# Hybrid attention/recurrence layer: attention's and the gates' loads on the GpSimd queue, tiles under store reused last, two heads' probability products at a time, the ranking held at the first pair

## The chip, the cores and the metric

The kernel runs on one core of a Trainium2 chip. The metric is device microseconds (us) of one execution, as a median over runs; the profile is of one further execution. The engines are named as in the profile: PE (matrix products), PEld (its weight loads), DVE (vector), ACT (scalar), POOL (GpSimd), SP (only issues transfers). ACT and POOL can issue transfers too; `SPq`, `ACTq` and `POOLq` in the profile are the issuing sides of these engines.

## What is computed

One layer over 512 tokens plus 16 prepended meta tokens, model width 2048, all in float32. Cut to what matters here:

```python
proj = rms_norm(x, norm_g) @ w_in                 # 2048 x 12368
(q_a, k_a, v_a, z_a, q_i, k_i, w_i, q_b, f_b, i_b, z_b, gates) = split(proj)
# branch A: an indexer scores keys, the best 128 per query are kept, 8 heads attend to them
score = einsum(relu(qi . ki), wi);  sel = top_k(score, 128)
o_a = softmax(q . k over sel) @ v;  y_a = o_a * silu(z_a)      # 8 heads, 4 key/value groups
# branch B: gated linear recurrence, 8 heads
y_b = rms_norm(hgrn2(silu(q_b), f, i_b)) * silu(z_b)
p = einsum('btnc,ncd->btnd', stack(y_a, y_b), w_branch)
out = x + sum(sigmoid(gates) * p, n) @ w_out
```

## The kernel before

**Products in three parts.** Each float32 operand is split into a high and a low part (`hi_lo`, L381: ACT copies the high part, DVE subtracts for the low one), and each product is three matmuls: high x high, high x low, low x high. In the profile `wh`/`wl` are the parts of a weight, `hH`/`hL` of the normed input, `yH`/`yL` of a branch's output.

**Stages.** First the indexer's columns and four of branch B's gate columns run as plain jobs (`pg`, about the first 196 us). Then pairs of column blocks run in a seven-product scheme (`run_pair`, L1306, with banks `px`, `py`, `pz`, `pw`), one pair in about 20 us. Seven operands per pair are prepared on the side: sums of weight blocks on DVE (`sum_1`, `sum_2`, L408) and by accumulating transfers on POOL (`sum_3`, `sum_4`, L419). The seven input operands include one, `t3`, that needs its own place in `hH`/`hL`: `place_t3` (L1286) copies it there when the last plain job has read them. Then 32 plain jobs multiply by `w_branch`: 16 for branch B (n=1), 16 for branch A (n=0), 24 matmuls each (`pg` again). The last stage multiplies by `w_out` with the seven-product scheme (`po`).

**Attention between the jobs.** The 8 heads of attention are worked off as side tasks between the matmuls of branch B's 16 jobs. `vs_task` (L791) prepares the meta tokens' values. `att_task(h)` (L851) loads a head's `qH`, `qL` and, for every second head, its group's four key/value tiles `kv`; forms the logits `plg`; adds the mask and takes the maximum on DVE (L895); takes the exponential and normalizes on ACT. It then starts `pv_task(h)` (L914): PE transposes blocks of probabilities (`ppt`), ACT and DVE split them (`pT`, `pTH`, `pTL`, `pS`), PE multiplies them with the values (`pov`). At its end a head is multiplied by its gate `za` and split into `yH[0,h]`, `yL[0,h]`, which the jobs of branch A read. A head's `pv_task` begins when those of all heads before it are done. Before the first job of branch A, `req_br` (L1557) runs the side tasks until all eight are done.

**What sets the order.** Nothing moves instructions after they are written. The Python code keeps an estimated clock per engine (`Core.at`, L57 on) and a list of tasks; `pump` (L222) is called after every few matmuls and steps any task whose time has come by that clock. Tasks have priorities; the ranking, `topk_task` (L679: 16 rounds for each of four query blocks), has number 6. Each engine takes its instructions in the written order, so an instruction that waits holds up all behind it on its engine. This goes for transfers as well: SP issues weight loads (`load_chunk`, L356), spills, the attention's loads and the gates' loads in one row.

**Memory.** 69 slots of 128 x 528 are handed out by `Slots.get`, which takes the free one whose last use by the estimated clock is the oldest. `Slots.put` (L167) frees a slot and notes that last use. A slot that is freed right after its store to DRAM was issued counts as last used by the computation before the store. The n=1 jobs' gates come back from DRAM (`load_gates`, L1468) into two weight tiles in turn; branch B's outputs come back by `load_y` (L1482), eight tiles, in the last pair.

Of the kernel before, what the change touches and what calls it, by code (L numbers as in the profile page):

```python
# [8 lines left out]
F32 = mybir.dt.float32  # L9
# [135 lines left out]
class Slots:  # L145
# [20 lines left out]

    def put(self, *aps):  # L167
        for a in aps:
            nm = a.tensor.name
            t = self.tag.pop(nm)  # L170
            self.last[t] = self.core.ac.get(nm, (0.0, "pe"))
            self.free.append(t)
# [9 lines left out]
def hybrid_kernel(ctx, tc, x, meta, vecs, w_in, rows, w_branch, w_out,  # L182
# [12 lines left out]

    tasks = []

# [24 lines left out]
    def pump(limit=3000.0):  # L222
        moved = True
        while moved:
            moved = False
            for t in list(tasks):
                now = E.clk["pe"]
                lim = limit if t.prio < 5 else 1200.0
                if t.t + MARGIN <= now and E.clk["dve"] < now + lim and E.clk["act"] < now + limit:
                    if not t.done and t.step():  # L230
                        moved = True
                        break
# [485 lines left out]
    def keep_out(moves, tiles, e, key):  # L718
        yield e
        for dst, src in moves:  # L720
            nc.sync.dma_start(dst, src if src.dtype == F32 else src.bitcast(F32))
        S.put(*tiles)
        stored.add(key)
# [67 lines left out]
    def vs_task():  # L791
        while len(stored) < 17:
            yield WAIT
        yield from room(8)
        vx3.extend((slot("vS", F32R), slot("pS", F32R), slot("v3")))
        vS, _, v3 = vx3
        nc.scalar.dma_start(v3[:, :512], v3d)
        vx = slot("vx")
        nc.scalar.dma_start(vx[:, :64], vxd)
        for t in vx3[:2]:  # L800
            E.pool([t], [], T // 2, lambda v: v.memset(t[:96, :512].bitcast(F32), 0.0))
# [15 lines left out]
    def spill(dst, s, e, key=None):  # L817
        yield e
        nc.sync.dma_start(dst, s[:, :512])
        S.put(s)  # L820
        if key:
            y_out.add(key)
# [28 lines left out]
    def att_task(h):  # L851
        g = h // 2
        while not vx3 or h and att.get(h - 1, 0) < 1 or not topk_done():
            yield WAIT
        yield from room(2 if g in kTH else 6, 6)
        if g not in kTH:
            for d, src, n in ((kTH, kd_[g][0], T), (kTL, kd_[g][1], T), (vH, vd_[g][0], 512), (vL, vd_[g][1], 512)):
                d[g] = slot("kv", F32R)
                nc.sync.dma_start(d[g][:, :n].bitcast(F32), src)
        qH, qL = slot("qH", F32R), slot("qL", F32R)  # L860
        for i, t in enumerate((qH, qL)):
            nc.sync.dma_start(t[:, :512].bitcast(F32), qd_[h][i])
        yield E.clk["pe"] + 7000.0
        while h and att[h - 1] < 2 or len(S.free) < 8:
# [23 lines left out]
        att[h] = 1  # L888
        yield e3
        col = lambda qt, i: sm[:, 4 * qt + i:4 * qt + i + 1]  # L890
# [10 lines left out]
        for qt in (3, 2, 1, 0):  # L901
            xs = ps[qt][:, :KQ[qt]]
            e = E.act(xs, xs, AF.Exp, bias=col(qt, 1), accum_out=col(qt, 2))
        yield e
        E.dve([sm], [sm], 4, lambda vv: vv.reciprocal(allc(3), allc(2)))
# [3 lines left out]
        att[h] = 2  # L909
        pv_tasks.append(spawn(pv_task(h, ps, e), 1))  # L910

    pv_tasks = []

    def pv_task(h, ps, e):  # L914
        g = h // 2
        gs = slice(128 * g, 128 * g + 128)
        for t in pv_tasks[:h]:
            while not t.done:
                yield WAIT
        yield e  # L920
        vS, pS, v3 = vx3
        po = yield from bank("pov")
# [17 lines left out]
        for b in (3, -1, 0, 1, 2):  # L940
# [14 lines left out]
            if b == 3:  # L955
                z = slot("za")
                nc.sync.dma_start(z[:, :512], zad[h])
            if b != 2:
# [15 lines left out]
        e = E.tt(z[:, :512], po, z[:, :512], OP.mult)  # L974
        B1.put(po)
        if h % 2 == 1:
            S.put(kTH[g], kTL[g], vH[g], vL[g])
# [328 lines left out]
    def run_pair(pr, nxt, late, last):  # L1306
# [3 lines left out]
        for i, (wn, tn, bn, on_) in enumerate(SEVEN):  # L1310
# [46 lines left out]
            if last:  # L1357
                if i == 1:
                    while len(y_out) < 8:
                        pump(1e9)  # L1360
                        if len(y_out) < 8:
                            E.clk["pe"] += 200
                    yr = load_y(0, 4)
                elif i == 3:
                    S.put(*hH[:8], *hL[:8])
                    yr += load_y(4, 8)
                    ysplit = split_y(yr, 1)
                elif i == 4:
                    S.put(*[t for k in range(8) for t in TB[k]["tiles"][:2]])
                elif i == 5:  # L1370
                    S.put(*[TB[k]["tiles"][2] for k in range(8)])
                elif i == 6:
                    S.put(*hH[8:], *hL[8:])
                    late.pop(0)()
                if i in (4, 5):
                    for _ in range(4):
                        next(ysplit, None)
# [90 lines left out]
    def load_gates(n, p):  # L1468
# [6 lines left out]
        for i in range(2):  # L1475
            nc.sync.dma_start(g[i][:, :512], gd[n][p + 8 * i])
            gate[n, p + 8 * i] = g[i]
# [3 lines left out]

    def load_y(a, b):  # L1482
        yr = slots("yr", b - a)
        for h in range(a, b):
            nc.scalar.dma_start(yr[h - a][:, :512], yd[h])
        return yr
# [58 lines left out]
    def d_gate(n, j, c0):  # L1545
        def f(g):
            E.act(g[:, c0:512], g[:, c0:512], AF.Sigmoid)
            nc.sync.dma_start(gd[n][j], g[:, :512])
            S.put(g)
        return f  # L1550
# [6 lines left out]
    def req_br(n, p):  # L1557
        def f():
            if p == 0:
                if n:  # L1560
                    load_gates(1, 0)
                else:
                    while len(pv_tasks) < 8 or not all(t.done for t in pv_tasks):
                        pump(1e9)
                        E.clk["pe"] += 200
            if p < 7:
# [9 lines left out]
    jobs[7].pre = lambda: spawn(consts(), 2)  # L1576
    jobs[-1].pre = lambda: (sum_1(jobs[ji]), sum_2(jobs[ji]))

# [105 lines left out]
    for k in E.clk:  # L1684
        E.clk[k] = max(E.clk[k], E.clk["pe"]) + (2500.0 if k in ("dve", "act") else 0.0)
    npair, late = 0, []
    first_out = min(i for i, j in enumerate(jobs) if j.kind == "out")
    for ji, job in enumerate(jobs[2:], 3):
# [5 lines left out]
        if job.kind == "pair":  # L1694
            npair += 1
            if npair == 1:
                for t in t_task:
                    finish(t)
                late += [lambda: place_t3(0), lambda: place_t3(4)]
            last = npair == len(pairs)  # L1700
# [17 lines left out]
        else:  # L1718
            b = B1.get("pg")
            parts = [(b[:job.ncols, :], slice(0, 512))]  # L1720
            if job.kind == "in":
                parts = [(b[:job.ncols, :].rearrange("p (a b) -> p a b", a=2), None)]
        for ch in job.chunks:
            split_upto(ch["prep"] + 2)
# [83 lines left out]
```

## Time and profile before

| | |
|---|---|
| median of 3 runs | 1540.3 us (1539.25 to 1540.68) |
| the profiled execution | 1538.31 us, of it the span from first to last instruction 1536.5 us |
| granted PE clock, mean | 0.996 |
| busy in the span | PE 1506.5, DVE 1177.3, ACT 683.3, POOL 156.9 us |
| transfers issued by POOL, by SP and by ACT | 52.52 MB (q0); 186.89 MB (q1); 8.69 MB (q10) |

How to read it: a row of a wait is "who waited on which line, for what: us in total, times, the longest". A row of a timeline is "start, duration, engine, line, operation, out<-in, count", and in brackets the idle time before it and what ended it. Busy times of PE overlap a little, since one matmul's modelled end lies behind the next one's start. "PEclk" is the share of full clock that was granted.

### The profile page before, as it was taken

How to read it: one execution, taken by the hardware profiler on the slowest of the kernel's cores; microseconds unless marked ns; L12 is line 12 of the kernel's file. 1: busy time of each engine (PE TensorE's matmuls, PEld its weight loads, DVE VectorE, ACT ScalarE, POOL GpSimd, SP SyncE). 2: the span in 40 equal slices, each digit the busy share in tenths (PEclk: the TensorE clock that was granted, in tenths of full speed). 3: DMA queues.
4: the chain of work that ended last, by engine and by line, in shares of the span. 5: the costliest groups of instructions: out<-in, count | busy, mean ns of one | idle time of the engine just before them, and what ended most of it. 6: DMA issues, size and time to landing. Idle time of an engine off the chain costs nothing.

```text
span 1536.5 us, 30975 instructions
## 1 busy us (share of the span) xinstructions
PE 1506.5 (98%) x12648; PEld 1423.1 (93%) x12648; DVE 1177.3 (77%) x1971; ACT 683.3 (44%) x1050; POOL 156.9 (10%) x162
## 2 busy tenths in 40 slices
PE   7999999999999999999999999999989999999998
PEld 6888899999999999999999999999987887889998
DVE  6799999999998778677768776886654555778775
ACT  5555444444444433443444344334465553334332
POOL 3100000001111101101000000000100000002222
PEclk9999999999999999999999999999999999999999
DMA  9323367777887855766676667566777543458873
GB/s 265 83 69 83 100 143 181 185 176 167 214 206 186 201 136 138 180 146 162 145 172 135 157 163 169 142 151 172 189 237 241 158 138 103 143 142 214 221 206 91
DMA packets 305999, 250.08 MB, mean 163 GB/s; under 512 B 13060, under 2 KB 268048, under 8 KB 305856
## 3 DMA queue, kind: packets, MB, share of 16 engines
q1 hardware_dynamic: 284448, 186.89, 41.6%
q0 software_dynamic: 14464, 52.52, 20.2%
q10 hardware_dynamic: 6944, 8.69, 1.7%
q8 instruction: 99, 1.62, 0.4%
q14 instruction: 44, 0.36, 0.1%
HBM read 168.00 MB, written 27.62 MB: 127 GB/s over the span
## 4 chain that ended last, share of the span: by engine, by line
PE 91%; DMA 3%; DVE 2%; ACT 2%; issue 2%; POOL 0%; SPq 0%; ACTq 0%; POOLq 0%; DVEq 0%
PE pg L93 20%; PE pz L91 15%; PE py L91 15%; PE px L91 14%; PE po L91 10%; PE pw L91 7%; PE phl L93 1%; PE psc L93 1%; PE plg L93 1%; PE pov L91 1%; PE pho L93 1%; DMA raw<-in_w_branch_dram 1%; DMA qL<-qd 1%; PE phs L93 1%; ACT wh L101 1%
## 5 line engine op out<-in xcount | busy, mean ns | idle before, releaser
L101 ACT ACTIVATE wh<-raw 128x1024 fp32r<-128x1024 f32 x304 | 322.3, 1060 | 479.1 <-PE pz L91 123.4
L107 DVE TENSOR_TENSOR wl<-raw,wh 128x1024 fp32r<-128x1024 f32 x302 | 371.5, 1230 | 142.2 <-ACT wh L101 140.6
L91 PE MATMUL px<-hH,wh 128*128 128x256 f32 (+1 forms) x672 | 193.8, 288 | 0.0
L91 PE MATMUL px<-hH,wl 128*128 128x256 f32 (+1 forms) x672 | 189.6, 282 | 0.0
L91 PE MATMUL px<-hL,wh 128*128 128x256 f32 (+1 forms) x672 | 189.1, 281 | 0.0
L101 ACT ACTIVATE wh<-sum 128x1024 fp32r<-128x1024 f32 x100 | 106.1, 1061 | 181.7 <-PE pw L91 72.6
L91 PE MATMUL po<-wh,mh 128*128 128x256 f32 x896 | 158.4, 280 | 0.5 <-DVE xq L107 0.5
L107 DVE TENSOR_TENSOR wl<-sum,wh 128x1024 fp32r<-128x1024 f32 x100 | 128.4, 1284 | 35.2 <-ACT wh L101 35.1
L91 PEld LDWEIGHTS po<-wh,mh 128*128 128x128 f32 x896 | 137.2, 189 | 0.8 <-DVE xq L107 0.7
L91 PEld LDWEIGHTS px<-hH,wh 128*128 128x128 f32 x672 | 126.4, 188 | 0.9
L91 PEld LDWEIGHTS px<-hL,wh 128*128 128x128 f32 x672 | 126.4, 188 | 0.0
L91 PEld LDWEIGHTS px<-hH,wl 128*128 128x128 f32 x672 | 126.4, 188 | 0.0
L91 PE MATMUL po<-wl,mh 128*128 128x256 f32 x448 | 125.5, 280 | 0.0
L91 PE MATMUL py<-tT,wh 128*128 128x256 f32 (+1 forms) x672 | 124.9, 285 | 0.0
L91 PE MATMUL pw<-tT,wh 128*128 128x256 f32 (+1 forms) x672 | 124.5, 284 | 0.0
L91 PE MATMUL pz<-tT,wh 128*128 128x256 f32 (+1 forms) x672 | 123.3, 283 | 0.0
L116 POOL DMA_DIRECT2D raw<-raw x50 | 43.2, 864 | 753.7 <-DVE sum L107 743.9
L91 PEld LDWEIGHTS py<-tT,wh 128*128 128x128 f32 x672 | 103.3, 188 | 0.5
L91 PEld LDWEIGHTS pw<-tT,wh 128*128 128x128 f32 x672 | 103.3, 189 | 0.2
L91 PEld LDWEIGHTS pz<-tT,wh 128*128 128x128 f32 x672 | 103.1, 188 | 0.2
L93 PE MATMUL pg<-yH,wh 128*128 128x512 f32 x256 | 102.7, 401 | 0.0
L93 PE MATMUL pg<-yH,wl 128*128 128x512 f32 x256 | 100.5, 393 | 0.0
(307 smaller groups left out, 3766.4 us busy)
## 6 DMA issues: line engine op xcount, KB each, us to landing
raw<-in_w_in_dram SPq DMA_DIRECT2D x192, 512.0 KB, 4.6
raw<-raw POOLq DMA_DIRECT2D x50, 512.0 KB, 5.3
raw<-sum POOLq DMA_DIRECT2D x50, 512.0 KB, 5.7
raw<-in_w_branch_dram SPq DMA_DIRECT2D x32, 512.0 KB, 4.7
raw<-in_w_out_dram SPq DMA_DIRECT2D x32, 512.0 KB, 4.6
gd<-g SPq DMA_DIRECT2D x32, 256.0 KB, 4.8
g<-gd SPq DMA_DIRECT2D x30, 256.0 KB, 3.0
x<-in_x_dram SPq DMA_DIRECT2D x16, 256.0 KB, 5.5
```

The costliest lines, as they stand in the source:

```text
L91: self.nc.tensor.matmul(out, lhsT, rhs, start=start, stop=stop, skip_group_check=True)
L93: self.nc.tensor.matmul(out, lhsT, rhs, start=start, stop=stop)
L101: self.nc.scalar.activation(out, in_, f, **kw)
L107: self.nc.vector.tensor_tensor(out, a, b, op=op)
L116: self.nc.gpsimd.dma_start(out, a, accum_op=OP.add)
```

## The change

- **Queues.** The attention's loads (`qH`, `qL`, `kv`, `za`, the meta tokens' `v3` and `vx`) and the gates' loads go from SP or ACT to POOL's queue; of `load_y`'s eight loads the first four stay on ACT and the other four go to POOL. A head's q is asked for ahead of its group's kv. The first gates of branch B (`load_gates(1, 0)`) are asked for at the end of the last pair.
- **Slots.** `put(..., late=9000.0)` counts a slot that is under a store as last used 9 us from now, so that `get` prefers others.
- **Two heads at a time.** There are two `pS` tiles, and a head's `pv_task` waits for the head before the last one only; the multiplication's end still keeps the order of heads. The written waits between a head's steps are longer: 10000 in place of 7000 (ns by the estimated clock) from its loads to its logits, 600 more ahead of the mask, 1200 ahead of the reciprocal, 1000 ahead of `pv_task`.
- **Branch A's start.** `req_br` waits for no head. The first two jobs of branch A run through the eight inner blocks together, and each block waits only for its own head.
- **First pair.** From the last plain job's start until the first pair's second product, tasks with a priority number over 5 are not stepped (`hold`); both halves of `place_t3` are written ahead of the pair and not after its first and second product.

```diff
-    def put(self, *aps):
+    def put(self, *aps, late=0.0):
...
-            self.last[t] = self.core.ac.get(nm, (0.0, "pe"))
+            w = self.core.ac.get(nm, (0.0, "pe"))
+            self.last[t] = (max(w[0], self.core.clk["pe"]) + late, "dma") if late else w
...
+                if t.prio > 5 and hold:
+                    continue
...
-        S.put(*tiles)
+        S.put(*tiles, late=9000.0)
...
-        vx3.extend((slot("vS", F32R), slot("pS", F32R), slot("v3")))
-        vS, _, v3 = vx3
-        nc.scalar.dma_start(v3[:, :512], v3d)
+        vx3.extend((slot("vS", F32R), slot("pS", F32R), slot("pS", F32R), slot("v3")))
+        vS, v3 = vx3[0], vx3[3]
+        nc.gpsimd.dma_start(v3[:, :512], v3d)
...
+        qH, qL = slot("qH", F32R), slot("qL", F32R)
+        for i, t in enumerate((qH, qL)):
+            nc.gpsimd.dma_start(t[:, :512].bitcast(F32), qd_[h][i])
...
-                nc.sync.dma_start(d[g][:, :n].bitcast(F32), src)
-        qH, qL = slot("qH", F32R), slot("qL", F32R)
-        for i, t in enumerate((qH, qL)):
-            nc.sync.dma_start(t[:, :512].bitcast(F32), qd_[h][i])
-        yield E.clk["pe"] + 7000.0
+                nc.gpsimd.dma_start(d[g][:, :n].bitcast(F32), src)
+        yield E.clk["pe"] + 10000.0
...
-        yield e3
+        yield e3 + 600
...
-        yield e
+        yield e + 1200
...
-        pv_tasks.append(spawn(pv_task(h, ps, e), 1))
+        pv_tasks.append(spawn(pv_task(h, ps, e + 1000), 1))
...
-        for t in pv_tasks[:h]:
-            while not t.done:
-                yield WAIT
+        while h > 1 and not pv_tasks[h - 2].done:
+            yield WAIT
...
-                nc.sync.dma_start(z[:, :512], zad[h])
+                nc.gpsimd.dma_start(z[:, :512], zad[h])
...
+        while h and not pv_tasks[h - 1].done:
+            yield WAIT
...
-                    yr = load_y(0, 4)
+                    yr = load_y(0, 4, nc.scalar)
...
-                    yr += load_y(4, 8)
+                    yr += load_y(4, 8, nc.gpsimd)
...
+                    load_gates(1, 0)
...
-            nc.sync.dma_start(g[i][:, :512], gd[n][p + 8 * i])
+            nc.gpsimd.dma_start(g[i][:, :512], gd[n][p + 8 * i])
...
-            if p == 0:
-                if n:
-                    load_gates(1, 0)
-                else:
-                    while len(pv_tasks) < 8 or not all(t.done for t in pv_tasks):
-                        pump(1e9)
-                        E.clk["pe"] += 200
...
-    jobs[-1].pre = lambda: (sum_1(jobs[ji]), sum_2(jobs[ji]))
+    jobs[-1].pre = lambda: (sum_1(jobs[ji]), sum_2(jobs[ji]), hold.append(1))
...
-                late += [lambda: place_t3(0), lambda: place_t3(4)]
+                place_t3(0)
+                place_t3(4)
+                late += [lambda: None, lambda: hold.clear()]
...
+        if job.kind == "br" and job.n == 0 and job.c0 in (0, 1024):
+            ahead.append((job, b))
+            if len(ahead) < 2:
+                continue
+            split_upto(ahead[1][0].chunks[0]["prep"] + 1)
+            for kt in range(8):
+                while (0, kt) not in yL or not pv_tasks[kt].done:
+                    pump(1e9)
...
+                for j, o in ahead:
+                    mm3(o, j.chunks[0], kt, kt, yH[0, kt][:, :512], yL[0, kt][:, :512], kt == 0, kt == 7)
+                    pump()
+            for j, o in ahead:
+                j.done(o)
+            continue
```

**What moves, place one: DVE at the first pair.** Before, from the first half of `place_t3` (`hL`) to the first pair's second product, whose subtraction from `py` is the row that begins with `p_`; MAX and MATCH_REPLACE are one round of the ranking, `tk` its work tile:

```order
L107 TENSOR_TENSOR hL_347<-t_148_1338,hH_346 128x264
L107 TENSOR_TENSOR hL_362<-t_148_1338,hH_361 128x264
L690 MAX m_0_2001<-tk_2000 128x8
L691 MATCH_REPLACE tk_2000<-m_0_2001,tk_2000 128x144
L690 MAX m_1_2009<-tk_2008 128x8
L691 MATCH_REPLACE tk_2008<-m_1_2009,tk_2008 128x272
L107 TENSOR_TENSOR p_253_2279<-p_253_2279,py_2298 128x256
L107 TENSOR_TENSOR wl_2330<-sum_26_2153,wh_2329 128x1024
L107 TENSOR_TENSOR hL_376<-t_105_1043,hH_375 128x264
```

Now, from the second half of `place_t3` on:

```order
L107 TENSOR_TENSOR hL_415<-t_236_2079,hH_414 128x264
L107 TENSOR_TENSOR hL_439<-t_236_2079,hH_438 128x264
L107 TENSOR_TENSOR wl_2252<-raw_2016,wh_2251 128x1024
L107 TENSOR_TENSOR wl_2284<-raw_1840,wh_2283 128x1024
L107 TENSOR_TENSOR p_253_2281<-p_253_2281,py_2292 128x256
L107 TENSOR_TENSOR wl_2320<-sum_26_2153,wh_2319 128x1024
L693 MAX m_0_2001<-tk_2000 128x8
L694 MATCH_REPLACE tk_2000<-m_0_2001,tk_2000 128x144
```

All eight `hL` stand ahead of the pair's weights, and nine rounds of the ranking, which stood between the last plain job and this subtraction, stand behind it.

**Place two: the queue that carries the first head's loads.** Before, on SP, the first head's loads among the loads of `w_branch` and the store of the gates:

```order
L363 DMA raw_13875<-in_w_branch_dram 128x8x128
L363 DMA raw_13908<-in_w_branch_dram 128x8x128
L859 DMA kv_13922<-kd_0_122 128x528
L859 DMA kv_13924<-kd_1_123 128x528
L859 DMA kv_13926<-vd_0_130 128x512
L859 DMA kv_13928<-vd_1_131 128x512
L862 DMA qH_13930<-qd_0_138 128x512
L862 DMA qL_13931<-qd_1_139 128x512
```

Now, on POOL, from the last accumulating transfer of the last pair on:

```order
L116 DMA raw_13559<-sum_190_13687 128x1024
...
L1490 DMA yr_13897<-yd_170 128x512
L800 DMA v_556_13909<-v3d 128x512
L802 DMA vx_13911<-vxd 128x64
L804 MEMSET vS_13906 96x512
L804 MEMSET pS_13907 96x512
L804 MEMSET pS_13908 96x512
L861 DMA qH_13916<-qd_0_138 128x512
L861 DMA qL_13917<-qd_1_139 128x512
L865 DMA kv_13920<-kd_0_122 128x528
L865 DMA kv_13922<-kd_1_123 128x528
```

The loads stand behind no weight load any more, but behind four `yr` loads, the meta tokens' loads and three fills. SP's row is 72 instructions shorter (473 to 401), POOL's 79 longer (167 to 246).

**Place three: PE at the end of attention.** Before, in head 6 (bank `pov_15281`), the second last:

```order
L91 MATMUL pov_15281<-pS_13760,vS_13759 128x512
L97 MATMUL ppt_15307<-ident,lg_14829 128x128
L97 MATMUL ppt_15307<-ident,lg_14827 128x128
L97 MATMUL ppt_15307<-ident,lg_14825 128x128
L91 MATMUL pov_15281<-pTH_15303,kv_14719 128x512
L91 MATMUL pov_15281<-pTL_15304,kv_14719 128x512
```

Now, with head 6 in bank `pov_15153` and the last head, 7, in `pov_15231`:

```order
L91 MATMUL pov_15153<-pTH_15224,kv_14810 128x384
L93 MATMUL pg_15211<-yH_13965,wh_14992 128x512
L93 MATMUL pg_15211<-yL_13966,wh_14992 128x512
L93 MATMUL pg_15211<-yH_13965,wl_14993 128x512
L93 MATMUL pg_15211<-yH_13969,wh_14992 128x512
L93 MATMUL pg_15211<-yL_13970,wh_14992 128x512
L93 MATMUL pg_15211<-yH_13969,wl_14993 128x512
L91 MATMUL pov_15231<-pS_13908,vS_13906 128x512
```

Before, heads 6 and 7 stood alone behind the last job of branch B. Now they alternate with each other and with that branch's fourteenth job, and two whole jobs (48 matmuls) stand behind the last head.

More of the change, by code (lines that the diff above doesn't have):

```diff
@@ L193, in hybrid_kernel @@
     B2 = Slots(E, pp, ["c0"], [128, 2, 512], None)
-    tasks = []
+    tasks, hold = [], []
     class Task:
@@ L793, in vs_task @@
             yield WAIT
-        yield from room(8)
-        vx3.extend((slot("vS", F32R), slot("pS", F32R), slot("v3")))
-        vS, _, v3 = vx3
-        nc.scalar.dma_start(v3[:, :512], v3d)
+        yield from room(9)
+        vx3.extend((slot("vS", F32R), slot("pS", F32R), slot("pS", F32R), slot("v3")))
+        vS, v3 = vx3[0], vx3[3]
+        nc.gpsimd.dma_start(v3[:, :512], v3d)
         vx = slot("vx")
-        nc.scalar.dma_start(vx[:, :64], vxd)
-        for t in vx3[:2]:
+        nc.gpsimd.dma_start(vx[:, :64], vxd)
+        for t in vx3[:3]:
             E.pool([t], [], T // 2, lambda v: v.memset(t[:96, :512].bitcast(F32), 0.0))
@@ L819, in spill @@
         nc.sync.dma_start(dst, s[:, :512])
-        S.put(s)
+        S.put(s, late=9000.0)
         if key:
@@ L916, in pv_task @@
         gs = slice(128 * g, 128 * g + 128)
-        for t in pv_tasks[:h]:
-            while not t.done:
-                yield WAIT
+        while h > 1 and not pv_tasks[h - 2].done:
+            yield WAIT
         yield e
-        vS, pS, v3 = vx3
+        vS, pS, v3 = vx3[0], vx3[1 + h % 2], vx3[3]
         po = yield from bank("pov")
@@ L1480, in hybrid_kernel, with load_y @@
     yH, yL = {}, {}
-    def load_y(a, b):
+    def load_y(a, b, q):
         yr = slots("yr", b - a)
         for h in range(a, b):
-            nc.scalar.dma_start(yr[h - a][:, :512], yd[h])
+            q.dma_start(yr[h - a][:, :512], yd[h])
         return yr
@@ L1548, in f @@
             nc.sync.dma_start(gd[n][j], g[:, :512])
-            S.put(g)
+            S.put(g, late=9000.0)
         return f
@@ L1685, in hybrid_kernel @@
         E.clk[k] = max(E.clk[k], E.clk["pe"]) + (2500.0 if k in ("dve", "act") else 0.0)
-    npair, late = 0, []
+    npair, late, ahead = 0, [], []
     first_out = min(i for i, j in enumerate(jobs) if j.kind == "out")
@@ L1722, in hybrid_kernel @@
                 parts = [(b[:job.ncols, :].rearrange("p (a b) -> p a b", a=2), None)]
+        if job.kind == "br" and job.n == 0 and job.c0 in (0, 1024):
[6 more added lines that the diff above has]
+                    pump(1e9)
+                    if (0, kt) not in yL or not pv_tasks[kt].done:
+                        E.clk["pe"] += 200
+                for j, o in ahead:
[4 more added lines that the diff above has]
+            continue
         for ch in job.chunks:
```

## The prediction, before the result was known

> **What bounds the kernel now.** First the page's busy times, then who PE waits for.
>
> ```profile
> PE 1506.5 (98%) x12648; PEld 1423.1 (93%) x12648; DVE 1177.3 (77%) x1971; ACT 683.3 (44%) x1050; POOL 156.9 (10%) x162
> PE pc L97 <- DMA vrow<-in_vecs_dram: 7.7, 1, 7.7
> PE plg L93 <- DMA qH<-qd: 7.3, 3, 4.4
> PE py L91 <- DVE p L107: 2.5, 1, 2.5
> PE pov L91 <- DVE pS L107: 2.1, 2, 1.2
> ...
> PE pz L91 <- DVE g L107: 0.7, 1, 0.7
> ```
>
> PE is the bound: 1506.5 of the span's 1536.5 us. Only its 30 us of idle time can go, and what follows from idle time. 7.7 us are the start, which the change doesn't touch. The waits of `plg` and `pov` are attention's, that of `py` is the first pair's. So I look at windows of these two places. Columns here: length, each engine's busy time and its instructions, then PEclk, DMA share, GB/s. First the windows for all instructions:
>
> ```profile
> 207.55:211.92 4.37, 4.37 (x26) 4.37 (x27) 4.33 (x10) 0.09 (x1) 0.00 (x0) 0.67 0.16 47
> 211.92:214.76 2.84, 2.84 (x26) 2.84 (x26) 2.81 (x6) 1.06 (x2) 0.43 (x1) 1.00 0.71 188
> 1131.59:1142.66 11.07, 6.67 (x42) 6.24 (x40) 8.66 (x15) 6.32 (x10) 0.00 (x0) 0.85 1.01 322
> ```
>
> These say what a stall costs beyond itself. The 24 matmuls right behind the 2.5 us wait took 4.37 us at a clock of 0.67; the next 24 took 2.84 at full clock. So that stall costs 2.5 + 1.5 = 4.0 us. Around the first logits the clock is 0.85 as well.
>
> Now attention. The same view for the `pg` matmuls of the jobs alone (their number is the first bracket), and the chain's row for one undisturbed head's logits:
>
> ```profile
> 1134.43:1160.98 26.55, 11.68 (x48) 8.79 (x48) 0.69 (x1) 0.00 (x0) 0.91 0.70 227
> 1160.98:1273.12 112.14, 83.75 (x336) 61.46 (x336) 9.58 (x14) 0.00 (x0) 0.99 0.54 172
> 1263.89:1273.12 9.23, 6.32 (x25) 4.21 (x24) 0.69 (x1) 0.00 (x0) 1.00 0.63 186
> 1273.12:1285.56 12.44, 0.16 (x2) 0.12 (x1) 0.68 (x1) 0.00 (x0) 1.00 0.13 42
> 1285.56:1373.94 88.38, 88.38 (x384) 71.88 (x384) 10.38 (x15) 0.00 (x0) 1.00 0.40 122
> 1170.43 1.94 PE plg L93 x15
> ```
>
> These give the work's floor. The last window holds 384 `pg` and nothing else: 88.38 / 384 = 0.230 us each. A head's 15 logit matmuls take 1.94. The third window is one whole head 5, transposes and products, with 24 `pg` between them (the PEld bracket; the 25th reaches over the edge): 9.23 - 24 x 0.230 = 3.7 us for a head. So 112.14 us in the middle hold 336 x 0.230 + 6 x 1.94 + 5.65 x 3.7 = 109.8 of work (two logits and a third of a head lie ahead of it): 2.3 lost. The first 26.55 us hold 48 x 0.230 + 2 x 1.94 + 1.3 = 16.2: 10.3 lost. In 12.44 us at the end the two heads that stand alone need 2 x 3.7 = 7.4: 5.0 lost. Together 17.6 us in attention.
>
> Why the first 26.55 us lose so much is read from SP's timeline and from PE's:
>
> ```profile
> 1126.39 3.20 SPq L363 DMA_DIRECT2D raw<-in_w_branch_dram  x2
> 1129.69 1.55 SPq L859 DMA_DIRECT2D kv<-kd  x2
> 1131.33 1.01 SPq L859 DMA_DIRECT2D kv<-vd  x2
> 1132.66 0.38 SPq L862 DMA_DIRECT2D qH<-qd  x1
> 1135.01 0.32 SPq L862 DMA_DIRECT2D qL<-qd  x1
> 1135.62 13.11 SPq L363 DMA_DIRECT2D raw<-in_w_branch_dram  x3
> 1149.15 0.81 SPq L1548 DMA_DIRECT2D gd<-g  x2
> 1150.01 2.35 SPq L1476 DMA_DIRECT2D g<-gd  x4
> 1152.45 0.38 SPq L862 DMA_DIRECT2D qH<-qd  x1
> ...
> 1138.99 0.81 PE L93 MATMUL plg<-kv,qH 128*128 128x264 f32 x2 [4.40 <-DMA qH<-qd]
> 1157.89 0.47 PE L93 MATMUL plg<-kv,qH 128*128 128x264 f32 x2 [2.70 <-DMA qH<-qd]
> ```
>
> Head 0's `qH` is issued at 1132.66, behind weight loads and kv, and PE waits for it until 1138.99. Head 1's stands behind three weight loads that hold SP for 13 us, then behind stores and gates; PE waits for it too.
>
> **The change, part by part.**
>
> *First pair.* The subtraction that PE waited for stood behind nine rounds of ranking and four `hL`; now it stands behind the eight `hL` and two `wl`.
>
> ```profile
> 200.62 1.35 ACT L101 ACTIVATE hH<-t 128x264 fp32r<-128x264 f32 x4
> 204.10 1.46 DVE L107 TENSOR_TENSOR hL<-t,hH 128x264 fp32r<-128x264 f32 x4
> 197.24 0.69 DVE L107 TENSOR_TENSOR hz<-pg,hz 128x512 f32<-128x512 f32 x1 [0.55 <-ACT hz L101]
> 207.32 1.22 DVE L107 TENSOR_TENSOR wl<-sum,wh 128x1024 fp32r<-128x1024 f32 x1
> ```
>
> From `hz`'s end at 197.9, eight `hL` take 2 x 1.46 = 2.9, to 200.8; the two `wl` 2 x 1.22, to 203.3; the subtraction is through at 203.7. PE needs it where it stopped: 207.55 less 2.53, 205.0. The first of these `wl` is ready at 202.0; PE comes to it one product ahead of that point, 205.0 - 2.84 = 202.2. So what is late next is that `wl`, by 0 to 1 us. ACT's eight `hH`, 2.7 us, run beside. I keep 0.3 of the 4.0: **-3.7** (bounds -2 to -4).
>
> *Ranking moved.* Nine rounds go to later, where DVE is as full. Today one such place stops PE (`pz` on DVE, 0.7): a power on POOL waits for DVE, and the accumulating transfer behind it comes late. In the new order two more rounds stand ahead of that power, some 2 us, and one copy less behind it. One more stall of that kind: **+1.0** (bounds -0.7, if even today's goes, and +4, two of 2.0).
>
> *First two heads.* POOL's pieces:
>
> ```profile
> L116 POOL DMA_DIRECT2D raw<-sum x50: 842/847/877, 202.1 to 1518.5; - x50
> DMA to landing us min/median/max: 4.5/5.4/8.0
> 1108.69 0.86 POOL L801 MEMSET pS<- 96x512 f32 x1
> 1126.00 1.06 ACT L101 ACTIVATE wh<-raw 128x1024 fp32r<-128x1024 f32 x1 [0.62 <-PE py L91]
> 1126.01 4.24 ACTq L1485 DMA_DIRECT2D yr<-yd  x4
> 1130.35 1.06 ACT L101 ACTIVATE wh<-raw 128x1024 fp32r<-128x1024 f32 x1 [3.29 <-DMA yr<-yd]
> ```
>
> The last pair's fourth product ends at 1126.0. It frees the tiles that the meta tokens' and most of head 0's loads go to; POOL's four `yr` go to tiles that are free earlier. From 1124 to 1126 on, POOL has `v3`, `vx`, three fills, `qH`, `qL` and two `kv`: six issues ahead of the last at 0.85 and three fills at 0.86, 7.7 us. The second `kv` is issued at 1131.7 to 1133.7, and lands 5.4 us later by POOL's median: 1137.1 to 1139.1. PE comes to it after three products of 2.84, four transposes and, new, twelve `pg` of 0.230: 1126.0 + 8.5 + 0.4 + 2.8 = 1137.7. So the wait is 0 to 1.4 us, or 4 at the longest landing, 8.0, which is no idle fear: the transfer engines' share here was 1.01. ACT's stop of 3.3 us for the second four `yr` goes, so the `yH` that the twelve `pg` need are split before 1134.9. Head 1's q now stands behind 4 kv and 4 gates only, 10 us ahead. I keep 1.5 of 10.3: **-8.8** (bounds -6 to -10.3).
>
> *Middle.* Waits for q and for `pS`; half of the 2.3 goes: **-1.1** (bounds +2, since ACT and DVE meet other orders, and -2.3).
>
> *End.* Heads 6 and 7 lie among jobs and two jobs follow. What covers their splits is 0.7 to 1.4 us of `pg` at a time, while one `pS` took ACT, ACT and DVE about 2 us; some of it may show. I keep 0.6 of 5.0: **-4.4** (bounds -2.5 to -5.0). Branch A's two interleaved jobs are the same 48 matmuls, and their wait for heads is met by the time that the two jobs before them take, 11 us; if attention were that late, each block would wait for its own head only.
>
> *The rest at nothing.* Slots under store reused last: the waits it removes are on ACT and POOL, none on PE. The longer written waits (600, 1200, 1000) are filled by `pg`; a second `pS` costs one fill of 0.86 on POOL. SP's weight loads lose 72 neighbours; none of them was late for PE.
>
> Sum: -3.7 + 1.0 - 8.8 - 1.1 - 4.4 = -17.0. The profiled execution took 1538.31 us, 1.8 more than its span and 2.0 less than the median; the terms are PE's and hold for both: 1540.3 - 17.0 = **1523.3**.
>
> **Rivals.** *The moved loads gain nothing.* They were late because the transfer engines were full (share 1.01, 322 GB/s), not because of the queue; the bytes are the same, and q is late again. Then only the first pair, the end and the ripple count: 1540.3 - 3.7 - 4.4 + 1.0 = 1533.2. Against it: head 1's wait came at a share of 0.70, behind 13 us of SP's own waits. By the Trainium skill, "DMA: Bandwidth & Descriptors", section "Issuing engines are not separate DMA queues", another issuing engine saves only the time of the issue, usually small. That rule leads to this rival; the trace speaks against it in so far as SP's row held q by waits, which the rule doesn't count. Chance 0.12.
>
> *POOL's queue becomes the bound: slower.* A load on POOL might have to wait for DVE's instructions on top of its own 0.85. From head 0 to the last head's q, POOL has some 60 pieces (16 q, 16 kv, 7 za, 16 gates, fills and first loads) in the time of 384 `pg` and eight heads, 88.4 + 8 x (1.94 + 3.7) = 133 us: 2.2 us each. With the 10 us of lead, and 17 + 3 us of gain to eat up, it gets slower from (133 + 30) / 60 = 2.7 us a piece. If each waits for two `wl` (0.85 + 2 x 1.22 = 3.3), the queue is 60 x 3.3 - 133 = 65 us late at the end, less 10 of lead: 1523.3 + 55 = 1578. Against it: the hundred issues of before kept to 0.84 to 0.93 while DVE was 77% busy. The Trainium skill, "SBUF — State Buffer", section "SBUF: two separate sides", has this trap: while DVE copies in a two-port mode, POOL can't write descriptors, and the queue stands. No trace here shows it; what ran on DVE beside those hundred issues was mostly two-input subtractions. Chance 0.06.
>
> *It isn't what it says.* Another early tile takes q's place as PE's wait (a `yH` split, a weight), so that the stalls come back one for one: within 0.2% of 1540.3. Nothing in the order points to it. Chance 0.04.
>
> **Numbers.** The forecast, 1523.3, has 0.78. Its own range, with about half of all bad bounds together, is 1518 (all stalls gone: -4.0 - 10.3 - 2.3 - 5.0 - 0.7) to 1530. To leave out no more than 2 in 10 the range goes a little into the first rival, 1531; beyond it lie most of that rival, the two others and a small tail of the forecast. A measurement tells 0.2%, 3.1 us, from no change: faster 0.78 + 0.12 = 0.90, within it 0.04, slower 0.06.
>
> **What would show it.** Right: no `py` wait on DVE near 205; no `plg` wait on `qH`, and on `kv` at most 2 us, at the first head; PEclk near 1 there; the stretch from the last pair's end to `po` about 225 us in place of 239.5; no `pov` wait over 1 us at the end; POOL's issues still at 0.85. Wrong: `plg` waits on POOL's loads at several heads, POOL issues over 2 us, or new waits of PE on DVE of over 4 us together between 215 and 460.

## The result, and the profile after

The changed kernel takes 1530.2 us (median; 1525.6 to 1531.4), the kernel before beside it 1539.8 (1537.5 to 1540.7). The ratio is 0.9935 (95% interval 0.9920 to 0.9951): by the ratio 10.0 us faster, 7.5 to 12.3. The forecast was 17.0 us. The profiled execution was the fastest of its runs, 1525.6 us, which matters below.

The page's busy times of the changed kernel, and who PE waits for in attention:

```profile
PE 1500.0 (98%) x12648; PEld 1417.8 (93%) x12648; DVE 1173.5 (77%) x1971; ACT 679.5 (45%) x1048; POOL 199.4 (13%) x241
```

```profile
PE ppt L97 <- ACT pT L101: 5.3, 2, 3.2
PE plg L93 <- DVE pS L107: 1.4, 1, 1.4
PE ppt L97 <- DVE pTL L107: 1.4, 2, 1.1
```

The waits that the prediction wanted gone are gone: 7.3 us of `plg` on `qH`, 2.5 of `py` on DVE, 2.1 of `pov` on `pS`. In their place stands a wait that the prediction did not have at all: `ppt`, the transposes of the probabilities, on ACT's `pT`, 5.3 us in two pieces.

**The first pair.** DVE's timeline of the changed kernel:

```profile
197.06 2.83 DVE L107 TENSOR_TENSOR hL<-t,hH 128x264 fp32r<-128x264 f32 x8
199.92 2.36 DVE L107 TENSOR_TENSOR wl<-raw,wh 128x1024 fp32r<-128x1024 f32 x2
202.20 0.41 DVE L107 TENSOR_TENSOR p<-p,py 128x256 f32<-128x256 f32 x1
```

The eight `hL` take 2.83 us (2.9 forecast), and the subtraction is through at 202.6, ahead of the 205.0 at which PE stopped for it before. The `wl` that was to be 0 to 1 us late is not.

**The first heads.** POOL's timeline, then a window over the first head:

```profile
1117.61 0.54 POOL L800 DMA_DIRECT2D v<-v3d  x1 [3.78 <-PE py L91]
1120.06 0.54 POOL L861 DMA_DIRECT2D qH<-qd  x1
1121.12 1.07 POOL L865 DMA_DIRECT2D kv<-kd  x2
```

```profile
1128.00:1145.00 17.00, 16.95 (x85) 13.81 (x83) 11.20 (x23) 13.51 (x26) 4.08 (x8) 1.00 1.09 329
```

An issue takes 0.54 us here, not the 0.85 of the accumulating transfers from which I took it, so both `kv` are issued by 1122.2, and PE is busy 16.95 of 17 us at full clock. The transfer engines are as full as before (share 1.09, 329 GB/s; before 1.01, 322), so the traffic is not what held q. Whether it was the queue alone, the experiments below ask.

**The stretch.** The prediction's measure was the time from the last pair's end to `po`, 225 us in place of 239.5. The tile views give the last start of `pz` and the first of `po`; before, then changed:

```profile
L91 PE MATMUL pz<-hH,wh x336: 277/282/389, 217.4 to 1134.1; 128*128 128x256 f32 x120, 128*128 128x264 f32 x48
L91 PE MATMUL po<-wh,mh x896: 274/281/387, 1373.9 to 1532.6; 128*128 128x256 f32 x180
```

```profile
L91 PE MATMUL pz<-hH,wh x336: 276/282/388, 212.7 to 1127.9; 128*128 128x256 f32 x120, 128*128 128x264 f32 x48
L91 PE MATMUL po<-wh,mh x896: 274/281/384, 1361.2 to 1520.0; 128*128 128x256 f32 x180
```

239.8 us became 233.3: of the 14.5 us that attention was to give, 6.5 came. No `pov` waits over 1 us at the end any more, so the rest was lost in between. There ACT's timeline has this (columns as always: start, length, and in brackets the idle time ahead with its releaser), with DVE's row that releases it and PE's that wait:

```profile
1194.09 0.74 ACT L101 ACTIVATE lg<-lg,small 128x528 f32<-128x528 f32 x1 [3.62 <-DVE small L121]
...
1196.34 0.47 ACT L101 ACTIVATE pTH<-ppt 128x384 fp32r<-128x384 f32 x1
1196.71 0.26 ACT L101 ACTIVATE pT<-ppt 128x128 f32<-128x128 f32 x1
...
1229.18 1.97 ACT L101 ACTIVATE lg<-lg,small 128x528 f32<-128x528 f32 x4 [1.81 <-DVE small L908]
1231.06 0.47 ACT L101 ACTIVATE pTH<-ppt 128x384 fp32r<-128x384 f32 x1
1231.43 0.26 ACT L101 ACTIVATE pT<-ppt 128x128 f32<-128x128 f32 x1
```

```profile
1193.88 0.17 DVE L121 TENSOR_SCALAR small<-small 128x4 f32<-128x4 f32 x1
```

```profile
1197.02 0.60 PE L97 MATMUL ppt<-ident,lg 128*16 128x128 f32 x4 [2.08 <-ACT pT L101]
1231.74 0.61 PE L97 MATMUL ppt<-ident,lg 128*16 128x128 f32 x4 [3.17 <-ACT pT L101]
```

A head's `att_task` writes its four masks for DVE and its four exponentials for ACT in one step. ACT takes its row in order. So the exponentials stand at the head of ACT's row, waiting for masks that DVE has queued behind other things, and the copies of the other head's transposes out of their banks (`pTH`, `pT`), the evacuations, stand behind them. At 1229.18 it is the four scalings that wait in the same way, for the reciprocal. ACT is 45% busy and still late.

**Theory after the result.** The shortfall is this: with two heads at a time, one head's softmax blocks the other's evacuations in ACT's row. The rivals: POOL's loads come late in the executions that were not profiled; or the moved loads gained nothing, and the gain came from elsewhere.

### The profile page after: what moved, and what is told of

Its sections match the earlier page's. It is cut to its first block, busy times and chain, and to the rows that moved or that the text cites. A ratio compares the mean times of both kernels' runs of the same rounds, so it can differ in the third digit from the quotient of the medians.

```text
span 1523.8 us, 30986 instructions
## 1 busy us (share of the span) xinstructions
PE 1500.0 (98%) x12648; PEld 1417.8 (93%) x12648; DVE 1173.5 (77%) x1971; ACT 679.5 (45%) x1048; POOL 199.4 (13%) x241
## 4 chain that ended last, share of the span: by engine, by line
PE 86%; issue 7%; ACT 2%; DVE 2%; POOL 1%; DMA 1%; ACTq 0%; POOLq 0%; DVEq 0%
PE pg L93 18%; PE pz L91 14%; PE py L91 14%; PE px L91 14%; PE po L91 10%; PE pw L91 7%; PE phl L93 1%; PE psc L93 1%; ACT lg L101 1%; PE pho L93 1%; PE pov L91 1%; PE phs L93 1%; DVE lg L898 1%; PE px L97 1%; DMA kv<-vd 1%
## 5 line engine op out<-in xcount | busy, mean ns | idle before, releaser
L93 PE MATMUL pg<-yL,wh 128*128 128x512 f32 x256 | 100.8, 394 | 0.0
```

What stands on the lines that cost most here:

```text
L93: self.nc.tensor.matmul(out, lhsT, rhs, start=start, stop=stop)
```

## The experiments

All ratios are to the kernel before, run beside each variant on the same chip. Differences in us are of medians unless said otherwise. The changed kernel itself ran on another chip than the later experiments; where a difference is taken across chips, the ratios give the same to within 0.6 us.

### The changed kernel again

No edit.

> The changed kernel once more, unaltered, beside the others. Its profiled execution took 1525.6 us, its other runs 1528.4 to 1531.4; the kernel before stood at 1537.5 to 1540.7. Theory (the middle of attention lost 8 to 10 us to new waits of PE for a ppt bank, where -1.1 was forecast): the same waits of ppt on ACT stand at the same heads, 5 us or more together, and the ratio to before is 0.992 to 0.995 again. Rival (POOL's loads come late in most executions, and the profiled one was a lucky one): a second profile shows plg waiting on qH or kv by 3 us or more. A third possibility is that the runs differ by chance all along the program: then no single wait differs by over 2 us between the two profiles.

1530.5 us (1527.0 to 1534.4), ratio 0.9944 (0.9928 to 0.9959). PE's rows and two windows (PEclk is the third number from the end), first of this execution, then the same windows of the first profile:

```profile
1198.58 1.02 PE L97 MATMUL ppt<-ident,lg 128*16 128x128 f32 x4 [2.09 <-ACT pT L101]
...
1233.73 1.02 PE L97 MATMUL ppt<-ident,lg 128*16 128x128 f32 x4 [3.16 <-ACT pT L101]
```

```profile
1232.00:1236.00 4.00, 2.27 (x11) 2.04 (x12) 0.56 (x1) 2.85 (x8) 0.00 (x0) 0.57 0.46 131
1236.00:1240.00 4.00, 4.00 (x17) 3.71 (x16) 1.70 (x3) 0.87 (x2) 0.00 (x0) 0.58 0.00 0
```

```profile
1232.00:1236.00 4.00, 4.00 (x30) 3.76 (x28) 1.91 (x5) 2.05 (x4) 0.00 (x0) 1.00 0.03 7
1236.00:1240.00 4.00, 4.00 (x25) 3.44 (x24) 2.47 (x10) 1.40 (x5) 0.00 (x0) 1.00 0.00 0
```

The waits are the same to 0.01 us, at the same heads, and no load is waited for: the rival of late loads falls. What differs is the clock behind the waits, 0.57 here and 1.00 there. PE was busy 1504.9 us here and 1500.0 there. So the first profile was the lucky one, by the clock and not by POOL: it paid 5.3 us for two waits, this one some 5 us more for the same two. The stretch shows it as well:

```profile
L91 PE MATMUL pz<-hH,wh x336: 276/282/388, 213.7 to 1129.0; 128*128 128x256 f32 x120, 128*128 128x264 f32 x48
L91 PE MATMUL po<-wh,mh x896: 274/281/389, 1365.9 to 1524.6; 128*128 128x256 f32 x180
```

It is 236.9 us here. This execution took 1530.2 us, the changed kernel's median; so in an ordinary execution attention gave not 6.5 us but 2.9.

### The loads back on the queues of before

```diff
-            nc.gpsimd.dma_start(t[:, :512].bitcast(F32), qd_[h][i])
+            nc.sync.dma_start(t[:, :512].bitcast(F32), qd_[h][i])
...
-        nc.gpsimd.dma_start(vx[:, :64], vxd)
+        nc.scalar.dma_start(vx[:, :64], vxd)
```

(The same for `kv`, `za`, the gates, `v3` and the last four `yr`.)

> The changed kernel with only its loads put back on the queues of before (q, kv, za and the gates on SP, v3, vx and the last four yr on ACT); order, holds and pairs of heads stay as changed. Theory (the queue is what made q late: the first-heads term of -8.8 was right): slower than the changed kernel by 6 to 10 us, with plg waiting on qH for some 7 us at the first two heads and the clock below 1 there. Rival 1 (the moved loads gain nothing, the transfer engines were full): within 2 us of the changed kernel, with no more wait on qH than it has. Rival 2 (POOL as a queue costs something in unprofiled executions): faster than the changed kernel by 2 us or more.

1533.8 us, ratio 0.9964 (0.9951 to 0.9978): 3.3 slower than the changed kernel, about half of the least expected. No wait on `qH` came back; another did:

```profile
1133.09 0.60 PE L97 MATMUL pvm<-ident,vx 128*16 128x128 f32 x4 [3.19 <-DMA vx<-vxd]
```

So the queue was not the only thing that mended q. The changed kernel also asks for q ahead of kv and 10 us ahead in place of 7.

### One head at a time in the changed kernel

```diff
-        while h > 1 and not pv_tasks[h - 2].done:
+        while h and not pv_tasks[h - 1].done:
```

> The changed kernel with one head's probability products at a time again: head h starts them when head h-1 is through, not head h-2; all else as changed, branch A's two interleaved jobs too. Theory (with two heads at a time one head's exponentials stand on ACT, waiting for masks and the reciprocal, ahead of the other's PSUM evacuations): the waits of ppt on ACT in the middle, 5 us or more, fall to under 2.5, while some of the end's 4 to 5 us come back: 2 to 6 us faster than the changed kernel in the middle and 2 to 5 slower at the end, in sum -3 to +2. Rival (two at a time is what hides the chain of a head's pS in the middle too): slower by 5 to 10 us, with pov waiting on pS at every head.

1527.8 us (1526.5 to 1529.6), ratio 0.9932 (0.9916 to 0.9947): 2.7 faster than the changed kernel by the medians, 1.9 by the ratios, whose intervals overlap. The long `ppt` waits are gone, although ACT stands ahead of its exponentials and scalings as long as before (30.0 and 11.8 us; with two heads 29.5 and 12.9): what stands behind them is no longer what PE waits for. At the end `pg` waits for the last two heads' `yH` instead:

```profile
1272.19 0.50 PE L93 MATMUL pg<-yH,wh 128*128 128x512 f32 x1 [1.34 <-ACT yH L101]
...
1281.49 0.50 PE L93 MATMUL pg<-yH,wh 128*128 128x512 f32 x1 [1.44 <-ACT yH L101]
```

Two heads at a time gain the changed kernel nothing, then: they cover the end and pay for it in the middle. That they cost it something, the intervals don't show.

### Two pauses in a head's softmax

```diff
-        E.ts(allc(1), allc(0), -1.0, None, OP.mult)
+        yield E.ts(allc(1), allc(0), -1.0, None, OP.mult) + 600
...
-        E.dve([sm], [sm], 4, lambda vv: vv.reciprocal(allc(3), allc(2)))
+        yield E.dve([sm], [sm], 4, lambda vv: vv.reciprocal(allc(3), allc(2))) + 600
```

> The changed kernel with two pauses written into a head's softmax: the step that writes the four masks on DVE ends there, and the four exponentials on ACT are written only when the planner has the last mask done plus 0.6 us; likewise between the reciprocal and the four scalings. Two heads at a time stay. Theory: ACT's rows no longer hold exponentials that wait ahead of evacuations; ACT's idle time before lg falls from 42 us to under 20, the waits of ppt on ACT fall from 5 to under 2 us, and the time falls by 4 to 8 us below the changed kernel. Rival 1 (DVE, not the place in ACT's row, is late): the waits move to ppt or pov on DVE and the time stays within 2 us. Rival 2 (a head's softmax takes longer now, and PE runs out of other heads' work at the end): slower by 2 us or more, with the stretch from the last pair's end to po longer than in the changed kernel.

1519.9 us (1517.9 to 1520.4), ratio 0.9873 (0.9858 to 0.9888): 10.6 faster than the changed kernel, where 4 to 8 were expected, and 20.2 than the kernel before. ACT's waits ahead of the exponentials and scalings in the changed kernel, then with the pauses:

```profile
ACT lg L101 <- DVE small L121: 29.5, 8, 5.0
ACT lg L101 <- DVE small L908: 12.9, 8, 1.9
```

```profile
ACT lg L101 <- DVE small L121: 12.0, 5, 3.6
ACT lg L101 <- DVE small L908: 5.2, 8, 1.3
```

And the stretch, as above:

```profile
L91 PE MATMUL pz<-hH,wh x336: 276/282/388, 215.2 to 1130.4; 128*128 128x256 f32 x120, 128*128 128x264 f32 x48
L91 PE MATMUL po<-wh,mh x896: 274/281/386, 1355.3 to 1514.5; 128*128 128x256 f32 x180
```

224.9 us: what the prediction had forecast for the change without them (225). No wait of PE in attention is over 0.5 us. This version beats both kernels.

### The first pair's edit alone, on the kernel before

```diff
-    jobs[-1].pre = lambda: (sum_1(jobs[ji]), sum_2(jobs[ji]))
+    jobs[-1].pre = lambda: (sum_1(jobs[ji]), sum_2(jobs[ji]), hold.append(1))
...
-                late += [lambda: place_t3(0), lambda: place_t3(4)]
+                place_t3(0)
+                place_t3(4)
+                late += [lambda: None, lambda: hold.clear()]
```

> The kernel before with the first pair's edit alone: ranking held, and both halves of the pair's first operand subtracted ahead of the pair. Theory (this term, -3.7, was right, and the ripple of the moved rounds, +1.0, was not there): 3 to 5 us faster than before, no py wait on DVE near 205, the clock at 1.00 there, and no new wait of PE on DVE of over 1 us between 215 and 460. Rival (the moved rounds give it back later): within 1.5 us of before, with pz or pg waiting on DVE or POOL by 1 us or more behind 215.

1534.6 us, ratio 0.9971 (0.9961 to 0.9982): 4.5 us (2.8 to 6.0) faster by the ratio. Its waits of PE hold no `py` on DVE and no `pz` on DVE. The ripple is not there.

### Lead and order alone

```diff
+        qH, qL = slot("qH", F32R), slot("qL", F32R)
+        for i, t in enumerate((qH, qL)):
+            nc.sync.dma_start(t[:, :512].bitcast(F32), qd_[h][i])
         if g not in kTH:
...
-        yield E.clk["pe"] + 7000.0
+        yield E.clk["pe"] + 10000.0
```

> The kernel before with q's two loads written ahead of the four of kv and 10 in place of 7 us of lead ahead of a head's logits; all loads stay on SP and ACT. The loads put back under the changed kernel cost 3.3 us and no wait on qH came back, so the step that gave the first heads' term to the queue is in doubt. Theory now (lead and order take away most of q's waits): 3 to 7 us faster than before, plg's waits on qH from 7.3 to under 2 us. Rival (the queue did it; q on SP still stands behind 13 us of weight loads): within 2 us of before, and plg waits 4 us or more for qH.

1539.0 us, ratio 1.0005 (0.9993 to 1.0016): no difference, although q is not waited for. Other waits took its place on PE:

```profile
1148.99 0.47 PE L97 MATMUL ppt<-ident,lg 128*128 128x128 f32 x1 [2.24 <-ACT lg L101]
...
1263.97 0.49 PE L91 MATMUL pov<-pT,v 128*128 128x128 f32 x2 [2.35 <-ACT pT L101]
```

The first head's stall moved from its logits to its scalings, and the end became worse: its waits of `pov` are 6.6 us together, before 3.2. The time is the rival's, the waits are the theory's: q's waits did go, and nothing came of it.

### The queues alone

The kernel before with the diff's `nc.gpsimd` for the loads, and nothing else of it.

> The kernel before with the loads' queues alone changed: q, kv, za, gates, v3, vx and the last four yr on POOL; kv stays ahead of q, the lead stays 7 us, heads one at a time. Theory (either measure, queue or lead, is enough for q; the prediction's mechanism): 5 to 9 us faster than before, waits on qH under 2 us. Rival 1 (the transfer engines were full, the queue doesn't matter): within 2 us of before, waits on qH of 4 us or more. Rival 2 (the fills and kv on POOL hold q as long as SP did): half the gain, 2 to 4 us, plg's first wait still on qH.

1539.0 us, ratio 0.9996 (0.9988 to 1.0005): no difference. POOL's timeline, and PE's row:

```profile
1118.65 1.09 POOL L1485 DMA_DIRECT2D yr<-yd  x2 [0.90 <-ACT p L101]
1132.76 1.07 POOL L1485 DMA_DIRECT2D yr<-yd  x2 [13.02 <-DMA gd<-g]
...
1135.93 0.54 POOL L862 DMA_DIRECT2D qH<-qd  x1
```

```profile
1143.53 0.81 PE L93 MATMUL plg<-kv,qH 128*128 128x264 f32 x2 [8.97 <-DMA qH<-qd]
```

POOL stops 13 us at its third `yr`: the tile for it is still being stored (`gd<-g`). All of head 0's loads stand behind, and PE waits 9.0 us for `qH`, twice as long as before the change.

### Tiles under store given back at once, in the changed kernel

```diff
-        S.put(*tiles, late=9000.0)
+        S.put(*tiles)
```

(The same for the two other stores.)

> The changed kernel with tiles under a store given back at once in the planner's order again (late is 0), all else as changed. Theory (the prediction put this edit at nothing: its waits are on ACT and POOL, none on PE): within 2 us of the changed kernel. Rival (the loads to POOL's queue meet tiles that a store still reads, POOL's row stands, and q or kv comes late): slower by 3 us or more, with plg waiting on loads.

1535.3 us, ratio 0.9973 (0.9965 to 0.9982): 4.8 slower than the changed kernel (4.5 by the ratios). POOL's row and PE's:

```profile
1128.71 0.52 POOL L804 MEMSET pS<- 96x512 f32 x1 [8.78 <-DMA gd<-g]
```

```profile
1136.16 0.36 PE L93 MATMUL plg<-kv,qH 128*128 128x264 f32 x1 [4.28 <-DMA kv<-kd]
```

Again a store's tile: the fill of the second `pS` stands 8.8 us ahead of q and kv. The edit that the prediction put at nothing is worth some 5 us here.

### Queues and tiles under store together, on the kernel before

The loads on POOL's queue and the later reuse of tiles under store, nothing else of the change.

> The kernel before with two parts of the change together: the loads on POOL's queue and tiles under a store reused last. Each alone has gained nothing or lost: in the kernel before with POOL's queue alone, POOL stood 13.0 us at its third yr, whose tile a gate's store still read, and head 0's qH came 9.0 us late; the changed kernel without the tile rule was 5 us slower. Theory (the two work only together: a queue in order is worth what its slowest tile allows): 5 to 9 us faster than before, POOL's longest wait between 1110 and 1136 under 4 us, waits on qH under 2 us. Rival (the lead of 10 us and q ahead of kv are needed as well): under 3 us faster, qH still waited for by 3 us or more.

1532.9 us, ratio 0.9955 (0.9943 to 0.9968): 6.9 us (4.9 to 8.8) faster by the ratio. `qH` is still waited for at the first head, 3.1 us, so the lead of 10 us may have some work left to do; POOL's longest stop ahead of it was 4.1 us. Neither expectation held whole: the gain is the theory's, the wait the rival's.

### The pauses alone, on the kernel before

The two pauses as above; one head at a time.

> The kernel before with the two pauses in a head's softmax alone; one head's products at a time, as before. Theory (the pauses mend what two heads at a time broke, and the kernel before lost only some 2 us in the middle): within 2.5 us of before, plg's waits on qH unchanged at 7 us. Rival (ACT's row was a bottleneck in the kernel before too, and the 10.5 us that the pauses brought to the changed kernel are no cost of two heads): faster by 5 us or more.

1531.5 us, ratio 0.9952 (0.9941 to 0.9964): 7.4 us (5.5 to 9.1) faster by the ratio. The rival was right: ACT's row was a bottleneck in the kernel before as well. ACT's waits there, and the `pg` matmuls (PEld's bracket) from the last pair's end to the end of head 0's products, before and with the pauses:

```profile
ACT lg L101 <- DVE small L121: 34.2, 8, 5.8
ACT lg L101 <- DVE small L905: 9.8, 7, 1.7
```

```profile
1134.43:1178.40 43.97, 25.25 (x102) 19.03 (x102) 2.73 (x4) 0.00 (x0) 0.92 0.68 222
```

```profile
1135.35:1169.30 33.95, 17.75 (x72) 13.27 (x72) 1.38 (x2) 0.00 (x0) 0.95 0.85 279
```

ACT stood 44 us ahead of exponentials and scalings in the kernel before, and PE felt none of it there, since branch products filled the time. But they were used up: head 0 was through after 102 of them, with the pauses after 72. The price was paid at the end, where the last two heads stood alone and 5.0 us were lost. With the pauses enough of them are left for the last head. The `pg` matmuls from its first transpose to its last product, with the pauses:

```profile
1270.30:1278.18 7.88, 5.08 (x20) 3.40 (x20) 0.20 (x1) 0.00 (x0) 1.00 0.33 102
```

Of the 20, 18 stand between its steps and two reach over the edge; before, none stood between the steps of the last two heads. No `pov` waits for `pS` any more. PE's waits on q fell as well, from three of 7.3 us to one:

```profile
PE plg L93 <- DMA qH<-qd: 5.2, 1, 5.2
```

The second head's logits come to PE when its q has landed.

### Pauses and one head at a time, in the changed kernel

Both edits shown above.

> The changed kernel with the pauses, and one head's products at a time. Theory (with ACT's row mended, what two heads at a time are worth is the end's cover, 4.4 us by the prediction): 3 to 6 us slower than the changed kernel with pauses alone (1519.9), with pov waiting on pT or pS, or pg on yH, near the last two heads. Rival (two heads at a time are worth nothing once the pauses are there): within 1.5 us of 1519.9.

1520.2 us, ratio 0.9875 (0.9862 to 0.9887); with the pauses and two heads 1519.9, ratio 0.9873. The rival was right: once ACT's row is mended, two heads at a time are worth nothing that these runs can tell from none. A little of what the theory named is there: `pov` waits for `pT`, 2.5 us in three pieces (0.5 with two heads), and the stretch is 226.4 us in place of 224.9.

### The first pause alone, in the changed kernel

The pause between masks and exponentials alone.

> The changed kernel with the first pause alone, between the masks and the exponentials; the scalings still follow the reciprocal in one step. Of the two long waits of ppt, 2.1 us stood behind exponentials that waited for masks and 3.2 us behind scalings that waited for the reciprocal. Theory (each pause takes its own wait, and a wait costs 1.7 to 2 times its length with the clock that follows): 4 to 6 us faster than the changed kernel, 4 to 6 slower than with both pauses, one ppt wait of about 3 us left. Rival (the masks are the whole of it, ACT idled 29.5 us for them and 12.9 for the reciprocal): within 2 us of 1519.9.

1521.6 us, ratio 0.9882 (0.9868 to 0.9896): 8.9 faster than the changed kernel (9.5 by the ratios). The rival held: the masks are nearly the whole of it, and the long wait behind the scalings goes with them. One wait of `ppt`, 1.6 us for a mask on DVE, is in its place.

## Why the prediction was right in direction and off in size

- **First pair (-3.7) and ripple (+1.0).** The first is right in mechanism and in size: from the profile of before to the second one of the changed kernel, both with 7.7 us of waiting at the start, the first `pz` moves from 217.4 to 213.7. The ripple has the wrong sign: from there to the last `pz` 1.4 us were gained. I built it on the 0.7 us wait of `pz` on DVE; that wait went away with the change and no other came. The other 0.7 is not traced. Together -2.7 forecast, -4.5 (2.8 to 6.0) measured alone.
- **First two heads (-8.8).** The waits on `qH` went, the clock there is 1.00, and POOL issues in 0.54 us. But the step that gave this to the queue failed. With the loads back on SP no wait on `qH` came back either, and the time rose by 3.3; POOL's queue alone gains nothing, lead and order alone gain nothing. On the kernel before the queue is worth 6.9, and only with an edit that I had put at nothing: "the waits it removes are on ACT and POOL, none on PE". The queue's gain depends on POOL not stopping at a tile under store; without the rule it stops 8.8 or 13.0 us ahead of the first head's loads. I had costed the edit by who waits in the kernel before, where POOL carried no loads of attention.
- **Middle (-1.1) and end (-4.4).** The step that failed worst. The end was covered as forecast. But the middle did not give 1.1; it lost 5.3 us in the waits of `ppt` on ACT, 2.0 to 2.8 in new waits of `plg` and `ppt` on DVE, and up to 5 more in the clock behind them. Two heads at a time, -5.5 forecast, gained nothing; that they cost 2.7 by the medians lies within the noise. I took the end's loss to be the length of a head's own chain, ACT, ACT and DVE, uncovered. Its cause stood earlier: exponentials that wait at the head of ACT's row, so that the branch products were used up by then. The 34.2 us of ACT's waits stood in the profile of before; the sum has no term for them, since ACT was 44% busy and not on the path.
- **The sum.** -4.5 - 6.9 + 2.7 = -8.7, measured -10.0 (7.5 to 12.3). Forecast: -2.7 - 8.8 - 5.5 = -17.0. The parts were measured on two kernels and one of them lies within the noise, so that they meet the whole is no proof. Lead and order in company, the longer written waits and branch A's start hold the rest, if any; only lead and order were run alone.
- **What was luck.** In the same two profiles 5.1 us are gained up to the last pair's end (1134.1 and 1129.0), where 2.7 were forecast, and 2.9 in the stretch behind it (239.8 and 236.9), where 14.3 were: attention, most of the forecast, gave a fifth of its part. The time lies within the range all the same, but not for the forecast's reasons. The forecast's own range ended at 1530; 1530.2 is in only because it was let out to 1531 on account of the first rival.
- **Rivals.** That the moved loads gain nothing falls as stated: with the transfer engines at a share of 1.09 nothing waits. In a form that I did not give it holds: on the queue alone they gain nothing (ratio 0.9996). The Trainium skill, "DMA: Bandwidth & Descriptors", section "Issuing engines are not separate DMA queues", says that another issuing engine saves only the time to issue. Here its price was what stood ahead in that engine's row: 13.0 us of waiting with one rule for tiles, 4.1 with the other. POOL as the bound did not show: every issue of q took 0.54 us with DVE at 77%.

What stays open: how the 10.6 us of the pauses divide between the waits themselves and the clock behind them in an ordinary execution, since only one profile of each kernel but the changed one was taken; why the lead of 10 us made the end of the kernel before worse; and what the longer written waits and branch A's start do by themselves.

## What to carry to other kernels

An engine that is half idle can still set the time, if it takes its row in order and what stands first waits for another engine: look at its own waits, and at what is queued behind them, before calling it off the path. Cover is a stock: a stall that other work hides uses that work up, and shows where the stock runs out, so a loss at the end may have its cause 100 us earlier. And an edit whose waits hurt nobody today must be costed again with the other edits in place.

## What the runs showed of the hardware

The same wait costs a different time from one execution to the next, by the granted clock behind it. The 2.5 us wait of `py` was followed by a clock of 0.67 in the profile of before. In the kernel with lead and order alone, whose first pair is that of before, it was followed by 1.00, with the same wait of 2.52 us. In three more kernels with this first pair (the queues alone, the queues with the tile rule, the pauses alone) the same wait was followed by a clock of 0.61 over 24 matmuls. The kernel with lead and order alone, the wait lying in the first row:

```profile
205.00:210.00 5.00, 2.48 (x21) 2.30 (x21) 4.93 (x15) 1.33 (x2) 0.00 (x0) 1.00 0.70 158
210.00:215.00 5.00, 5.00 (x44) 5.00 (x44) 4.93 (x11) 2.13 (x2) 0.49 (x1) 1.00 0.39 110
```

A wait of 3.2 us was followed by 0.57 to 0.58 in one execution of the changed kernel and by 1.00 in another, worth some 5 us together with the wait of 2.1. The Trainium skill, "TensorE: Matmul & The Clock Gate", section "Part 1: The HAM clock gate", has a window of about 3.4 us that runs freely and does not start with the work; that would make the outcome a matter of phase. The runs agree with that in kind, though waits of 2.1 and 2.5 us, shorter than the window, were enough to lower the clock. The kernel with the pauses, which has no wait over 0.5 us in attention, may be steadier as well as faster: its four runs lie within 2.5 us of each other, the six of the changed kernel beside it within 7.3. So few runs suggest it and don't show it.
